# Seven products instead of eight in seven down-projection chunks of a decoder layer

## The chip, the cores and the metric

The kernel runs on one core of a Trainium2 chip. The metric is device time in microseconds (us) of one execution, the median of several; lower is better. Beside the timed runs there is one profiled execution, in which every instruction's start and duration is recorded. PE is TensorE (the matrix engine), PEld its weight loads, DVE is VectorE, ACT is ScalarE, POOL is GpSimd, SP is SyncE, which here issues the weight loads from memory.

## The reference

One decoder layer over 256 tokens of width 2048 in 32-bit floats: two groups of attention heads, an output projection, and an MLP with squared ReLU. Cut to what matters:

```python
h = rms_norm(x, norm1_g)
proj = h @ w_in                      # 2048 -> 6152: q, k, v of both groups, 8 forget logits
...                                  # forgetting attention, dilated attention
mixed = concatenate([rms_norm(y_a, outnorm_a_g), rms_norm(y_b, outnorm_b_g)])
x = x + mixed @ w_out                # 2048 -> 2048
h = rms_norm(x, norm2_g)
x = x + square(relu(h @ w_mlp_in)) @ w_mlp_out     # 2048 -> 8192 -> 2048
return rms_norm(x, final_norm_g)
```

The MLP holds the largest share of the arithmetic: 2 x 2048 x 8192 weights against 256 tokens.

## The kernel before

**Arithmetic.** Every large product is done in three terms. A 32-bit operand is split into a high part (a copy in the type float32r) and a low part, the rest. A product is then high x high + low x high + high x low, three TensorE instructions that add up in PSUM. For each step of weights ScalarE copies the raw weights into the high tile `whi` (line 178), and VectorE subtracts to get the low tile `wlo` (line 179).

**Chunks and steps.** The work on TensorE is a list of chunks (lines 111 to 128). A chunk is 512 output columns over up to 16 feature tiles of 128. First come 12 chunks of q, v and k, then 8 of the output projection, then the MLP in four rounds (r = 0 to 3). Each round has four up chunks `u` that make 2048 hidden features, then four down chunks `d` that multiply these by 2048 rows of the down weights and add the result to the residual `xs`. A step is two feature tiles of one chunk. A raw load brings four feature tiles (1 MB) into one of four `wraw` buffers.

**Two forms of product.** In q, k and u chunks (`turned_product`, line 327) the weights are loaded into the array as 128x128 blocks and 256 tokens of activations are streamed: 12 products of 256 columns per feature tile. In v, o and d chunks (`product`, line 319, lines 323 to 325) the activations of one 128-token tile are loaded and 512 weight columns are streamed: 2 token tiles x 3 terms = 6 products of 512 columns per feature tile. In the last chunk the second token tile is done in two halves of 256 columns.

**Order.** The loop at the end (lines 780 to 793) writes out the order by hand. Before the products of step i it issues the split of step i + 3 (`LEAD`), so the four buffers of `wsplit` hold the current step and the three next; then the products of step i, and after each of the two feature tiles the side work that was filed for that place (`at`, `run_side`). Side work includes the drains: `drain_u` (line 620) takes relu on ScalarE, the square on VectorE and splits the hidden activations into `hT_hi`, `hT_lo` (the memory of `big_hi`, `big_lo` in the profile). `drain_d` adds a finished down chunk to `xs` with one VectorE instruction per token tile (`add_down`, line 648); in the last round it also sums squares on ScalarE and multiplies by the final gain. The gain row `gf` uses the memory of `relT` and is loaded by `load_gf` in the last round's first down chunk. The last chunk (`last_chunk`) and `finish` end the kernel.

**PSUM.** There are eight banks of 512 columns: four named `acc` for chunks (two per chunk), two `sc` and two `tr` that attention uses and that stand empty in the MLP.

Of the kernel before, what the change touches and what calls it, by code (L numbers as in the profile page):

```python
# [19 lines left out]
P = 128  # L20
# [22 lines left out]
LINE, NEAR, HIGH, LOW, GATED = 64, 8, 24, 56, 48  # L43
TURNED = "qku"
# [29 lines left out]
def kernel(  # L74
# [32 lines left out]
    dram = ctx.enter_context(tc.tile_pool(name="dram", bufs=1, space=DRAM))  # L107
    ctx.enter_context(tc.manual_schedule())
# [14 lines left out]
    ROUNDS = D_FF // D_MODEL  # L123
    for r in range(ROUNDS):
# [6 lines left out]
    steps, last_slot = [], {}  # L131
    for ci, (what, key, w, r0, c0, cols, kts) in enumerate(chunks):
        for s in range(kts // 2):
            steps.append((ci, s))
        last_slot[what, key] = 2 * len(steps) - 1

    raws, splits = {}, {}

    def load(i):
        if i >= len(steps) or steps[i][1] % 2 or (steps[i][0], steps[i][1] // 2) in raws:  # L140
            return
        ci, s = steps[i]
        _, _, w, r0, c0, cols, _ = chunks[ci]
        t = wraw.tile([P, 4, CW + NH], F32, name="raw")
        src = w[r0 + s * 256:r0 + s * 256 + 512, c0:c0 + cols].rearrange("(k p) c -> p k c", p=P)
        raws[ci, s // 2] = t
        if i == 0:
            return t, src
        n = 2 if i == 2 else 4
        for k in range(0, 4, n):  # L150
            nc.sync.dma_start(t[:, k:k + n, :cols], src[:, k:k + n])

    def split(i, j0=0, n=2):
        if i >= len(steps):
            return
        if j0:
            return split_rows(i, j0, n)
        ci, s = steps[i]
        if ci == len(chunks) - 1 and s < 4:
            hi, lo = (a[:, 4 * s:4 * s + 4, :].rearrange("p (k j) s -> p k (j s)", k=2) for a in (aT_hi, aT_lo))  # L160
        else:
            what, cols = chunks[ci][0], chunks[ci][5]
            high, low = (HIGH, LOW) if what in TURNED else (NEAR, NEAR) if cols == CW else (GATED, HIGH - NEAR)
            hi, lo = (
                wsplit.tile([P, 2 * CW + LINE], F32R, name=n)[:, b:b + 2 * cols].rearrange("p (j c) -> p j c", j=2)
                for n, b in (("whi", high), ("wlo", low))
            )
        splits[i] = (hi, lo)
        split_rows(i, j0, n)

    def split_rows(i, j, n):
        ci, s = steps[i]
        hi, lo = (a[:, j:j + n, :] for a in splits[i])
        t = raws[ci, s // 2][:, 2 * (s % 2) + j:2 * (s % 2) + j + n, :chunks[ci][5]]
        cols = t.shape[2]
        step = cols // 2 if i == j == 0 else cols
        for c in range(0, cols, step):
            nc.scalar.activation(hi[:, :, c:c + step], t[:, :, c:c + step], AF.Copy)  # L178
        nc.vector.tensor_tensor(lo, t, hi.bitcast(F32), op=ALU.subtract)  # L179
# [42 lines left out]
    pick_sb = two.tile([P, RW], F32, name="pr")[:N_BUCKETS + 1]  # L222
# [12 lines left out]
    gcat = one.tile([P, TB, P], F32R, name="gcat")  # L235
# [108 lines left out]
    def products(i, j):  # L344
        ci, s = steps[i]
        what, key, _, _, _, cols, kts = chunks[ci]
        kt = 2 * s + j
        if what in TURNED:
            return turned_product(ci, i, j, kt, kts)
        a = operands(what, key)  # L350
        if cols > CW:
            return gated_products(ci, i, j, kt, kts, a)
        if kt == 0:
            accs[ci] = [psum.tile([P, CW], F32, name="acc", bufs=4) for _ in range(TB)]
        go, end = kt == 0, kt == kts - 1
        for t in range(TB):
            product(accs[ci][t], a, kt, t, splits[i], j, slice(0, CW), go, end)

# [18 lines left out]
    lf = two.tile([P, 2, 3 * P], F32R, name="p")  # L377
# [30 lines left out]
    gate_s = one.tile([P, SEQ], F32R, name="gate_s")  # L408
    gate_t = one.tile([P, SEQ], F32R, name="gate_t")
# [19 lines left out]
    relT = one.tile([P, NH, SEQ], F32, name="relT")  # L429
    rel_d = dram.tile([NH, RW], F32, name="rel_d")  # L430

    def rel_row():
        p = psum.tile([P, 512], F32, name="sc")
        nc.tensor.matmul(p[:NH, :RW], relx, pick_sb, start=True, stop=True)
        row = two.tile([P, RW], F32, name="neg")[:NH]
        nc.vector.tensor_copy(row, p[:NH, :RW])
        nc.gpsimd.dma_start(rel_d, row)
# [16 lines left out]
    def drain_v(g, ci):  # L454
        acc = accs.pop(ci)
        vh = one.tile([P, TB, CW], F32R, name="v_hi")
        vl = one.tile([P, TB, CW], F32R, name="v_lo")
# [12 lines left out]
    rows1 = one.tile([P, SEQ], F32, name="rows1")  # L470
# [11 lines left out]
    def drain_qk(g, what, ci, half):  # L482
        if half == 0:
            qkv[g, what] = one.tile([P, 2, 4, SEQ], F32R, name=what)
# [15 lines left out]
    def decay_of(hd):  # L500
        decay[hd] = two.tile([P, SEQ], F32R, name="gate_h")
# [6 lines left out]
    def scores(g, h):  # L508
# [25 lines left out]
        neg = two.tile([P, 3 * P], F32, name="neg")  # L534
        pr = two.tile([P, 3 * P], F32, name="pr")
# [19 lines left out]
    def turn_probs(g, h):  # L555
# [4 lines left out]
        parts = two.tile([P, 2, 3 * P], F32R, name="p")  # L560
# [3 lines left out]
    sq = [one.tile([P, SEQ], F32, name=f"sq{k}") for k in range(2)]  # L564
    seen = [0, 0]

    def values(g, h):
# [13 lines left out]
        s = sq[kind] if first else two.tile([P, SEQ], F32, name="sqt", bufs=1)  # L581
# [38 lines left out]
    def drain_u(c, ci):  # L620


        acc = accs.pop(ci)
        for half in range(2):
            h = two.tile([P, CW], F32, name="nat")
            nc.scalar.activation(h, acc[half], AF.Relu)
            nc.vector.tensor_tensor(h, h, h, op=ALU.mult)
# [4 lines left out]
            )  # L632

    gf = relT.rearrange("p h s -> p (h s)")
# [4 lines left out]
    def load_gf():  # L639
        nc.sync.dma_start(  # L640
            gf, bass.AP(tensor=final_norm_g.tensor, offset=final_norm_g.offset, ap=[[0, P], [1, D_MODEL]])
        )
# [4 lines left out]

    def add_down(acc, t, cs, n):
# [4 lines left out]
        if n is not None:  # L653
            unused = two.tile([P, CW], F32, name="nat")
            unused, xc, total = unused[:, :cs.stop - cs.start], xs[:, t, cs], ssq3[:, t, n:n + 1]
            if cs.stop < D_MODEL:
                nc.scalar.activation(unused, xc, AF.Square, accum_out=total)
                put_gain(t, cs)
            else:
                nc.vector.tensor_tensor_reduce(unused, xc, xc, 1.0, 0.0, ALU.mult, ALU.add, total)  # L660

    def put_gain(t, cs):
        nc.vector.tensor_tensor(xs[:, t, cs], xs[:, t, cs], gf[:, cs], op=ALU.mult)
# [51 lines left out]
    for ci, (what, key, *_rest) in enumerate(chunks[:-1]):  # L715
# [33 lines left out]
        elif what == "u":  # L749
            at(e, drain_u, key[1], ci)  # L750
        else:
            at(e, drain_d, *key, ci)
            if key == (ROUNDS - 1, 0):
                at(e - 8, load_gf)
# [27 lines left out]
    done = 10  # L782
    for i in range(final):
        if i:
# [39 lines left out]
```

## Time and profile before

| what | value |
|---|---|
| timed runs, median of 3 (range) | 1104.29 us (1103.9 to 1106.22) |
| profiled execution, first to last instruction | 1214.1 us |
| granted TensorE clock in the profile, mean | 0.850 of full speed |
| PE busy | 1201.8 us (99%) |
| VectorE busy | 655.5 us (54%) |
| ScalarE busy | 521.1 us (43%) |
| moved from and to memory | 209.17 MB, mean 172 GB/s |

The profiled execution's own time is its span; no other time is given for it. It is longer than the timed runs. In the rows of the profile `out<-in` names the tiles that an instruction writes and reads, `L340` is line 340 of the kernel before, and `x768` counts instructions. A matmul's duration (some 290 ns for 256 columns) is longer than its share of the array, since matmuls overlap; the pace is read from the starts of successive ones.

### The profile page before, as it was taken

The numbers are of one execution on the slowest core, as the hardware profiler recorded it, in microseconds if no ns is written. First come the engines' busy times: TensorE is split into PE (matmuls) and PEld (weight loads), VectorE is DVE, ScalarE is ACT, GpSimd is POOL, SyncE is SP. The second block draws the span as 40 slices with busy tenths as digits, with TensorE's granted clock in tenths as the row PEclk, the third lists the DMA queues.
The fourth block names the chain that finished last, engine by engine and source line by source line (L and its number), as shares of the span: only waits on it lengthen the run. The fifth ranks groups of instructions, "written<-read, shape, count | busy, mean of one in ns | idle before, by whom it ended". The sixth has DMA issues, their size and how long they took to land.

```text
span 1214.1 us, 17573 instructions
## 1 busy us (share of the span) xinstructions
PE 1201.8 (99%) x7373; PEld 1070.3 (88%) x7373; DVE 655.5 (54%) x837; ACT 521.1 (43%) x687; POOL 27.3 (2%) x42
## 2 busy tenths in 40 slices
PE   9999999999999999999999999999999999999997
PEld 8999898998987799987789997779998779998776
DVE  5666656556566655544544455445545444555563
ACT  5454535445444544443334443334444333444341
POOL 0010200000000000000000000000000000000000
PEclk8888888888888888888888888888888888888887
DMA  8664553544544455555555545555655555545541
GB/s 300 200 209 139 169 178 112 190 160 139 184 153 165 148 174 173 161 187 175 176 175 175 173 170 187 179 170 158 194 183 178 174 173 173 174 147 222 187 139 70
DMA packets 105387, 209.17 MB, mean 172 GB/s; under 512 B 3971, under 2 KB 5084, under 8 KB 105180
## 3 DMA queue, kind: packets, MB, share of 16 engines
q1 hardware_dynamic: 104412, 206.59, 51.6%
q8 instruction: 57, 0.93, 0.3%
q0 software_dynamic: 304, 1.06, 0.2%
q10 hardware_dynamic: 592, 0.40, 0.1%
q14 instruction: 22, 0.18, 0.0%
HBM read 205.93 MB, written 2.11 MB: 171 GB/s over the span
## 4 chain that ended last, share of the span: by engine, by line
PE 99%; DMA 0%; DVE 0%; issue 0%; ACT 0%; POOL 0%; ACTq 0%; DVEq 0%
PE acc L340 48%; PE acc L324 16%; PE acc L323 16%; PE acc L325 16%; PE tr L275 1%; PE sc L575 1%; PE sc L531 0%; PE tr L559 0%; DMA xs<-in_x_dram 0%; PE sc L527 0%; PE sc L577 0%; PE sc L323 0%; PE sc L324 0%; PE sc L325 0%; PE sc L521 0%
## 5 line engine op out<-in xcount | busy, mean ns | idle before, releaser
L179 DVE TENSOR_TENSOR wlo<-raw,whi 128x1024 fp32r<-128x1024 f32 (+2 forms) x382 | 464.0, 1223 | 416.9 <-ACT whi L178 414.8
L178 ACT ACTIVATE whi<-raw 128x1024 fp32r<-128x1024 f32 (+2 forms) x383 | 398.7, 1051 | 475.0 <-PE acc L340 230.1
L340 PE MATMUL acc<-aT_hi,whi 128*128 128x256 f32 x1536 | 450.5, 294 | 0.0
L340 PE MATMUL acc<-aT_hi,wlo 128*128 128x256 f32 x1536 | 446.3, 291 | 0.0
L340 PE MATMUL acc<-aT_lo,whi 128*128 128x256 f32 x1536 | 445.7, 291 | 0.0
L340 PEld LDWEIGHTS acc<-aT_hi,whi 128*128 128x128 f32 x1536 | 306.0, 199 | 1.5 <-ACT p L261 0.7
L340 PEld LDWEIGHTS acc<-aT_lo,whi 128*128 128x128 f32 x1536 | 304.8, 199 | 0.4
L340 PEld LDWEIGHTS acc<-aT_hi,wlo 128*128 128x128 f32 x1536 | 304.9, 199 | 0.0
L324 PE MATMUL acc<-whi,big_lo 128*128 128x512 f32 (+1 forms) x632 | 262.4, 415 | 0.0
L323 PE MATMUL acc<-whi,big_hi 128*128 128x512 f32 (+1 forms) x632 | 262.2, 415 | 0.0
L325 PE MATMUL acc<-wlo,big_hi 128*128 128x512 f32 (+1 forms) x632 | 260.6, 412 | 0.0
L323 PEld LDWEIGHTS acc<-whi,big_hi 128*128 128x128 f32 x632 | 121.6, 192 | 36.1
L325 PEld LDWEIGHTS acc<-wlo,big_hi 128*128 128x128 f32 x632 | 121.6, 192 | 35.9
L324 PEld LDWEIGHTS acc<-whi,big_lo 128*128 128x128 f32 x632 | 121.7, 193 | 34.6
L323 PE MATMUL acc<-whi,aT_hi 128*128 128x512 f32 (+1 forms) x144 | 54.7, 380 | 0.0
L324 PE MATMUL acc<-whi,aT_lo 128*128 128x512 f32 (+1 forms) x144 | 54.1, 376 | 0.0
L325 PE MATMUL acc<-wlo,aT_hi 128*128 128x512 f32 (+1 forms) x144 | 54.1, 376 | 0.0
L262 DVE TENSOR_TENSOR big_lo<-nat,big_hi 128x512 fp32r<-128x512 f32 x32 | 22.2, 692 | 22.4 <-ACT big_hi L261 22.4
L650 DVE SCALAR_TENSOR_TENSOR xs<-acc,rstd2sq,xs 128x512 f32<-128x512 f32 (+1 forms) x33 | 24.2, 734 | 16.2 <-PE acc L325 16.2
L325 PEld LDWEIGHTS acc<-wlo,aT_hi 128*128 128x128 f32 x144 | 27.7, 192 | 5.5
L323 PEld LDWEIGHTS acc<-whi,aT_hi 128*128 128x128 f32 x144 | 27.9, 194 | 5.2
L324 PEld LDWEIGHTS acc<-whi,aT_lo 128*128 128x128 f32 x144 | 27.9, 194 | 5.1
(167 smaller groups left out, 508.4 us busy)
## 6 DMA issues: line engine op xcount, KB each, us to landing
raw<-in_w_mlp_in_dram SPq DMA_DIRECT2D x64, 1024.0 KB, 5.3
raw<-in_w_mlp_out_dram SPq DMA_DIRECT2D x64, 1024.0 KB, 5.1
raw<-in_w_in_dram SPq DMA_DIRECT2D x42, 1024.0 KB, 5.0
raw<-in_w_out_dram SPq DMA_DIRECT2D x16, 1024.0 KB, 5.1
raw<-in_w_in_dram SPq DMA_DIRECT2D x4, 1040.0 KB, 8.1
xs<-in_x_dram SPq DMA_DIRECT2D x3, 512.0 KB, 9.8
raw<-in_w_in_dram SPq DMA_DIRECT2D x2, 512.0 KB, 5.7
big_lo<-rel_d POOLq DMA_DIRECT2D x1, 1024.0 KB, 7.0
```

Source lines behind the costliest of these rows:

```text
L178: nc.scalar.activation(hi[:, :, c:c + step], t[:, :, c:c + step], AF.Copy)
L179: nc.vector.tensor_tensor(lo, t, hi.bitcast(F32), op=ALU.subtract)
L262: nc.vector.tensor_tensor(lo, src, hi.bitcast(F32), op=ALU.subtract)
L275: nc.tensor.transpose(p[:, j * SEQ + t * P:j * SEQ + (t + 1) * P], xs[:, t, c:c + P], ident)
L323: nc.tensor.matmul(acc, xh, hi[:, j, cols], start=go, stop=False, skip_group_check=True)
L324: nc.tensor.matmul(acc, xl, hi[:, j, cols], start=False, stop=False, skip_group_check=True)
L325: nc.tensor.matmul(acc, xh, lo[:, j, cols], start=False, stop=end, skip_group_check=True)
L340: nc.tensor.matmul(acc, w[:, j, b * P:(b + 1) * P], a[:, kt, :], start=kt == 0 and b % 2 == 0 and n == 0, stop=kt == kts - 1 and n == 2, s ...
L575: nc.tensor.matmul(y[:, :SEQ], v[:, 0, dims], p[:, m, :SEQ], start=n == 0, stop=False, skip_group_check=True)
L650: nc.vector.scalar_tensor_tensor(xs[:, t, cs], acc[:, :cs.stop - cs.start], rstd2sq[:, t:t + 1], xs[:, t, cs], op0=ALU.mult, op1=ALU.add)
```

## The change

Seven of the 16 down chunks are computed by Strassen's scheme in its variant with 15 additions: d(0,0), d(1,0), d(2,0) and d(0,1), d(1,1), d(2,1), d(3,1). In these chunks four feature tiles, 256 tokens and 512 columns make a unit. It is cut into halves: two feature tiles (k1, k2), two token tiles (lower, upper), two column halves of 256. Where the plain form makes eight products of halves, the new form makes seven, with sums and differences of weight halves and of activation halves as operands. Each of these is again done in three terms.

A unit has four steps. **near** takes the k2 weights as they are (two products), **first** the left half of the k1 weights (one), **odd** two differences of weight halves (two), **even** two more (two). The differences are made by VectorE in a tile `both`: one instruction of 1024 elements at near, and two of 512 in place after odd has been split. The sums of activations are made once per up chunk by VectorE in place (`mix_activations`, four instructions of 256) and are split into `mix_hi`, `mix_lo` (`split_mixed`). The square in `drain_u` moves from VectorE to ScalarE.

The seven products add up in four banks, the two `sc` and the two `tr`, and `drain_seven` adds them to `xs` in four parts.

The order of steps changes. The units of d(r-1,0) are interleaved with the second halves of the up chunks of round r, one unit for each. Within a round d(r,3) comes first, then the units of d(r,1), each with two plain steps of d(r,2) between its steps; in the last round d(3,0) and d(3,3) follow as plain chunks.

Buffers: the attention tiles move into a pool of their own, which is closed where the MLP begins. Its memory then holds a fifth pair of split buffers, `mix_hi`, `mix_lo`, `both`, one small pair for first, and later the gain row. Splits are issued as far ahead as five large buffers (and one small) allow, and raw loads as soon as one of the four raw buffers is spent. `load_gf` moves to after the drain of d(3,1). In the last chunk three steps instead of four use the memory of `aT_hi`, `aT_lo`. The diff, cut to its core:

```diff
+    def mixed(ci, unit, behind):
+        b, a, t13, t24 = ((ci, 2 * unit, sub) for sub in ("near", "first", "odd", "even"))
+        return [b, a, t13, behind[0], t24] + behind[1:]
+
+    for r in range(ROUNDS):
+        for c in range(4):
+            mine = plain(index["u", (r, c)])
+            steps += mine[:4] + (mixed(index["d", (r - 1, 0)], c, mine[4:]) if r else mine[4:])
+        late = [index["d", (r, c)] for c in range(4)]
+        if r < ROUNDS - 1:
+            steps += plain(late[3])
+        for unit in range(4):
+            steps += mixed(late[1], unit, plain(late[2])[2 * unit:2 * unit + 2])
+        if r == ROUNDS - 1:
+            steps += plain(late[0]) + plain(late[3])
...
+    def split_seven(i):
+        ci, s, sub = steps[i]
+        t = raws[ci, s // 2][:, :, :CW]
+        half = CW // 2
+        if sub == "near":
+            both = sums_of[ci, s] = late_tiles["pool"].tile([P, 2, CW], F32, name="both")
+            nc.vector.tensor_tensor(halves(both), t[:, :, half:].rearrange("p (f k) c -> p f k c", f=2),
+                                    halves(t[:, :2]), op=ALU.subtract)
+        if sub == "first":
+            hi, lo = (late_tiles["pool"].tile([P, CW + LINE], F32R, name=n)[:, b:b + CW]
+                      for n, b in (("fhi", NEAR), ("flo", NEAR)))
+            src = t[:, :2, :half]
+        else:
+            hi, lo = part_tiles(i, 2 * CW, NEAR, NEAR)
+            src = t[:, 2:] if sub == "near" else sums_of[ci, s]
+        hi, lo = (a.rearrange("p (k c) -> p k c", k=2) for a in (hi, lo))
+        splits[i] = (hi, lo)
+        nc.scalar.activation(hi, src, AF.Copy)
+        nc.vector.tensor_tensor(lo, src, hi.bitcast(F32), op=ALU.subtract)
+        if sub == "odd":
+            a, b = src[:, :, :half], src[:, :, half:]
+            nc.vector.tensor_tensor(a, t[:, 2:, half:], a, op=ALU.subtract)
+            nc.vector.tensor_tensor(b, t[:, 2:, :half], a, op=ALU.subtract)
+            spent.add((ci, s // 2))
...
+    def seven_products(i, j):
...
+        todo = {
+            "near": ((one_, 0, h, k2, lower), (one_, half, m, k2, lower)),
+            "first": ((three, 0, h, k1, lower),),
+            "odd": ((two_, half, m, k2, upper), (four, 0, m, k1, upper)),
+            "even": ((three, half, m, k1, lower), (two_, 0, h, k2, upper)),
+        }[sub]
...
+            for x, (a, w) in enumerate(((ah, hi), (al, hi), (ah, lo))):
+                nc.tensor.matmul(acc, a[:, k, tokens], w[:, j, n * half:(n + 1) * half], start=fresh and x == 0,
+                                 stop=s == KT // 2 - 2 and j == 1 and x == 2, skip_group_check=True)
...
-            nc.vector.tensor_tensor(h, h, h, op=ALU.mult)
+            nc.scalar.activation(h, h, AF.Square)
...
+    def mix_activations(c):
+
+        a, b = kept[c]
+        (a11, a21), (a12, a22) = ((x[:, :, :P], x[:, :, P:]) for x in (a, b))
+        nc.vector.tensor_tensor(a22, a21, a22, op=ALU.add)
+        nc.vector.tensor_tensor(a21, a11, a21, op=ALU.subtract)
+        nc.vector.tensor_tensor(a11, a22, a11, op=ALU.subtract)
+        nc.vector.tensor_tensor(a12, a12, a11, op=ALU.subtract)
...
+        if part == 0:
+            s = late_tiles["pool"].tile([P, 2, half], F32, name="copies")
+            late_tiles["copies"] = s
+            nc.scalar.activation(s[:, 0], three[:, left], AF.Copy)
+            nc.scalar.activation(s[:, 1], four[:, left], AF.Copy)
+            nc.vector.tensor_tensor(rest, rest, s[:, 0], op=ALU.add)
+            add(0, cs, one_)
+        elif part == 1:
+            add(0, cs, three)
+            add(0, slice(cs.start + half, cs.stop), two_[:, right])
+        elif part == 2:
+            nc.vector.tensor_tensor(rest, rest, late_tiles["copies"][:, 1], op=ALU.add)
+            add(1, cs, two_)
+        else:
+            add(1, cs, rest[:, None, :].to_broadcast([P, 2, half]))
...
+            at(e + 2, mix_activations, key[1])
+            at(e + 4, split_mixed, key[1])
+        elif ci in seven:
+            for part in range(4):
+                at(e + 1 + 2 * part, drain_seven, *key, ci, part)
+            if key[0] == ROUNDS - 1:
+                at(e + 7, load_gf)
+                for c in (1, 2):
+                    for t in range(TB):
+                        at(e + 11 + 2 * c + t, put_gain, t, slice(c * CW, (c + 1) * CW))
...
+    def free_tiles(i):
+        live = [steps[n][2] for n in range(i, done + 2) if not (steps[n][0] == len(chunks) - 1 and steps[n][1] < 3)]
+        return len([n for n in live if n != "first"]) <= 5 and live.count("first") <= 1
...
+        if i >= mlp_start:
+            load_more()
+            while free_tiles(i) if i + LEAD < final else done < upto.get(i, i + LEAD):
+                done += 1
+                split(done)
+                load_more()
+            for j in range(2):
+                products(i, j)
+                run_side(2 * i + j)
+            continue
```

More of the change, by code (lines that the diff above doesn't have):

```diff
@@ L163, in split @@
             high, low = (HIGH, LOW) if what in TURNED else (NEAR, NEAR) if cols == CW else (GATED, HIGH - NEAR)
[L164 to L167, printed above, removed]
+            hi, lo = (a.rearrange("p (j c) -> p j c", j=2) for a in part_tiles(i, 2 * cols, high, low))
         splits[i] = (hi, lo)
@@ L559, in turn_probs @@
             nc.tensor.transpose(p[:, j * P:(j + 1) * P], pr[:, j * P:(j + 1) * P], ident)
-        parts = two.tile([P, 2, 3 * P], F32R, name="p")
+        parts = mix.tile([P, 2, 3 * P], F32R, name="p", bufs=2)
         split_psum(parts[:, 0], parts[:, 1], p[:, :3 * P])
         turned[g, h] = parts
-    sq = [one.tile([P, SEQ], F32, name=f"sq{k}") for k in range(2)]
+    sq = [mix.tile([P, SEQ], F32, name=f"sq{k}") for k in range(2)]
     seen = [0, 0]
```

149 lines of the change are left out of this document (115 added, 34 removed).

## The prediction

> **What bounds the kernel now.** I read the page first (busy times, granted clock, chain), then the waits, then two stretches of the MLP side by side, then the groups of instructions by shape, then the timeline at single places. The page:
>
> ```profile
> span 1214.1 us, 17573 instructions
> PE 1201.8 (99%) x7373; PEld 1070.3 (88%) x7373; DVE 655.5 (54%) x837; ACT 521.1 (43%) x687; POOL 27.3 (2%) x42
> PE 99%; DMA 0%; DVE 0%; issue 0%; ACT 0%; POOL 0%; ACTq 0%; DVEq 0%
> ```
>
> TensorE is busy 1201.8 of 1214.1 us and carries 99% of the chain that ended last. A busy PE need not be at its peak, so I look at pace. In the chain of waits, and in windows over the third round (its four up chunks, then its four down chunks) and over three other stretches (columns: us, then busy us and instructions of PE, PEld, DVE, ACT, POOL, then granted clock, DMA share, GB/s):
>
> ```profile
> 627.47 96.33 PE acc L340 x768
> ...
> 100.00:200.00 100.00, 100.00 (x692) 93.75 (x692) 61.98 (x116) 47.90 (x86) 8.19 (x9) 0.85 0.47 156
> 600.00:700.00 100.00, 100.00 (x690) 93.61 (x689) 48.98 (x46) 39.85 (x42) 0.00 (x0) 0.85 0.57 177
> 627.47:723.80 96.33, 96.33 (x769) 96.33 (x769) 47.85 (x47) 40.72 (x45) 0.00 (x0) 0.85 0.55 176
> 723.80:820.13 96.33, 96.33 (x386) 73.82 (x386) 46.93 (x43) 35.67 (x36) 0.00 (x0) 0.85 0.53 173
> ```
>
> Four up chunks are 768 products of 256 columns in 96.33 us: 0.12543 us each. Four down chunks are, by the code, 4 x 96 = 384 products of 512 columns, also in 96.33 us: 0.25086 us each, exactly twice. Time goes by columns streamed, at one clock (0.85), with no visible charge per instruction or per weight load. The timeline of the last chunk, second token tile, shows the form that the change uses (activations loaded, 256 weight columns streamed); first and last of its 96 products:
>
> ```profile
> 1193.24 0.30 PE L323 MATMUL acc<-aT_hi,big_hi 128*128 128x256 f32 x1
> ...
> 1205.17 0.28 PE L325 MATMUL acc<-wlo,big_hi 128*128 128x256 f32 x1
> ```
>
> (1205.17 - 1193.24)/95 = 0.1256 us: the same pace. So fewer streamed columns mean less time, as long as split weights are ready. That they are now, the waits show (us in total, times, longest; the first three are all that PE has, none in the MLP):
>
> ```profile
> PE tr L479 <- DVE nat L478: 1.3, 1, 1.3
> PE tr L275 <- DMA xs<-in_x_dram: 1.2, 1, 1.2
> PE sc L242 <- DVE relx L219: 1.2, 1, 1.2
> ...
> DVE wlo L179 <- ACT whi L178: 414.8, 312, 2.1
> ACT whi L178 <- PE acc L340: 230.1, 129, 2.1
> ACT whi L178 <- PE acc L324: 222.3, 124, 2.4
> SPq L151 <- DVE wlo L179: 1032.4, 180, 9.7
> ```
>
> Everything behind PE waits for PE: ScalarE for a free split buffer, VectorE for ScalarE, the load queue for VectorE.
>
> **The removal.** A unit is four feature tiles of one chunk. Plain: 4 x 2 token tiles x 3 terms = 24 products of 512 columns, 24 x 0.25086 = 6.02 us. As seven products: near 12, first 6, odd 12, even 12 = 42 of 256 columns, 42 x 0.12543 = 5.27 us. Saved 0.7526 us; 7 chunks x 4 units = 28 units: **21.07 us** of profile time. PE gets 28 x 18 = 504 instructions more, each with a weight load; by the two paces above these are free.
>
> **The added work on VectorE and ScalarE.** Prices, from groups by shape, and from the timeline:
>
> ```profile
> L179 DVE TENSOR_TENSOR wlo<-raw,whi 128x1024 fp32r<-128x1024 f32 x370 | 451.5, 1229 | 412.5 <-ACT whi L178 410.8 <-DMA pk<-in_pack_dram 0.5
> L650 DVE SCALAR_TENSOR_TENSOR xs<-acc,rstd2sq,xs 128x512 f32<-128x512 f32 x31 | 23.2, 750 | 10.7 <-PE acc L325 10.6
> L262 DVE TENSOR_TENSOR big_lo<-nat,big_hi 128x512 fp32r<-128x512 f32 x32 | 22.2, 692 | 22.4 <-ACT big_hi L261 22.4
> L627 DVE TENSOR_TENSOR nat<-nat 128x512 f32<-128x512 f32 x32 | 22.0, 688 | 11.1 <-ACT nat L626 11.1
> ...
> L178 ACT ACTIVATE whi<-raw 128x1024 fp32r<-128x1024 f32 x370 | 387.6, 1057 | 466.7 <-PE acc L340 229.7 <-PE acc L324 222.3 <-issue 7.7
> L261 ACT ACTIVATE big_hi<-nat 128x512 fp32r<-128x512 f32 x32 | 20.3, 633 | 26.1 <-DVE nat L627 26.1
> L626 ACT ACTIVATE nat<-acc 128x512 f32<-128x512 f32 x32 | 18.9, 590 | 21.1 <-PE acc L340 21.1
> ...
> 1205.49 0.48 DVE L650 SCALAR_TENSOR_TENSOR xs<-acc,rstd2sq,xs 128x256 f32<-128x256 f32 x1 [4.21 <-PE acc L325]
> 1206.61 0.41 DVE L663 TENSOR_TENSOR xs<-xs,relT 128x256 f32<-128x256 f32 x1
> ```
>
> VectorE per mixed unit: both 1.229, four low parts of near, odd, even (3 x 1.229) and first (0.692), two in-place differences (2 x 0.688) = 6.98 us, against 2.46 for a plain unit. ScalarE: 3 x 1.057 + 0.633 = 3.80, against 2.11. The strided differences are not in the trace; they lie between the plain 128x1024 row (1.229) and twice the row that reads PSUM (2 x 0.750 = 1.50 for 1024). I take 1.229, since both are SBUF to SBUF in runs of 256.
>
> The tightest place is the second chunk of a round interleaved with two plain steps of the third. PE per unit: 5.27 + 2 x 3.01 = 11.29 us. VectorE: 6.98 + 2.46 = **9.44**; ScalarE 5.92. Among up chunks: PE 24.08 + 5.27 = 29.35; VectorE 8 x 1.229 + 6.98 + the drain (low parts 2 x 0.692, mixing 4 x 0.41, mixed low parts 2 x 0.692; the squares go to ScalarE) = 21.2; ScalarE 8 x 1.057 + 3.80 + 2 x 0.590 + 6 x 0.633 = 17.2. A seven-product drain costs VectorE 4 x 0.75 + 3 x 0.48 = 4.4 us, not 1.5. Over the MLP VectorE gains 28 x 4.52 + 16 x 1.65 + 7 x 2.9 = 173 us, to about three quarters of the stretch. All of it lies beside PE as long as the lead over PE holds. That lead, in a down chunk (ScalarE, then VectorE):
>
> ```profile
> 738.64 1.06 ACT L178 ACTIVATE whi<-raw 128x1024 fp32r<-128x1024 f32 x1 [1.95 <-PE acc L324]
> ...
> 739.73 1.22 DVE L179 TENSOR_TENSOR wlo<-raw,whi 128x1024 fp32r<-128x1024 f32 x1 [1.78 <-ACT whi L178]
> ```
>
> PE frees a buffer at 738.6; it is refilled at 740.95 and used three steps later, at 738.6 + 3 x 3.01 = 747.6: 6.7 us to spare. Afterwards five buffers cover the five large operands of a unit. Near, freed 1.5 us into a unit, has its high part at 2.6 and its low part (both ran earlier) at about 3.8, and is used at 11.29: 7.5 us to spare. The plain steps are tightest, 6 us. A drain waits for a step whose buffer the next split needs as well, so it holds nobody back for longer than its own 4.4 us. Cost: nothing; if the lead were gone, see the rivals.
>
> **Moves and waits.** Loads: two megabyte loads per 11.29 us where it was one per 6.02; both chunks share four raw buffers. The final gain is now loaded after the second chunk's drain, behind the raw loads on SP's queue, and its first reader on VectorE comes three plain steps (9 us) later:
>
> ```profile
> raw<-in_w_mlp_out_dram SPq DMA_DIRECT2D x64, 1024.0 KB, 5.1
> relT<-in_final_norm_g_dram SPq DMA_DIRECT2D x1, 1024.0 KB, 8.4
> ```
>
> 8.4 against 9 us: at worst a wait of a few us on VectorE with low parts queued behind it, inside the 6 us of lead. The sc and tr banks that hold the seven products are drained during the five plain steps (15 us) before the next unit needs them. Attention's tiles move to a pool whose memory the MLP takes over; they were last read eight output chunks earlier. The tail (1205.3 to 1214.1) and the head keep their instructions. I take 0 for all of these, with 0 to 2 us for the range.
>
> **Sum.** 1214.1 - 21.07 = 1193.0 us of profiled span. No longer time is given for the profiled execution. The timed runs (1103.9 to 1106.22) are shorter than its span: median/span = 0.9096. PE is 99% of the span, so this can only be a faster PE; read as clock, 0.85/0.9096 = 0.93. The saving scales to 19.2 us, **1085.1 us**. Bounds: unscaled 21.1 (1083.2); at full clock 21.07 x 0.85 = 17.9 (1086.4). Other engines do not speed up with PE: the tight unit becomes 11.29 x 0.9096 = 10.27 us against VectorE's 9.44, still 8% free.
>
> The Trainium skill ("TensorE: Matmul & The Clock Gate", section "Wait — 56ns, not 53.3ns?") gives each warm matmul a fixed cost of about 2.5 ns beside its columns, which speaks against replacing long products by more short ones. By it 504 more products would cost 1.3 us, an estimate, and the time would be about 1086.3. The trace disagrees, at 0.85 clock: 0.25086 is exactly twice 0.12543.
>
> **Rivals.**
>
> *VectorE falls behind in the tight stretches.* For: only 8% is free there, and the strided forms and nine handovers per unit have no row. Against: 6 to 7 us of lead at each entry. If its work there costs 15% more, 10.86 against 10.27, the 16 units lose 0.59 each, 9.4 us, the lead hiding none: 1094.5. Chance 0.14.
>
> *The lead is lost, and ScalarE and VectorE work in turn.* Place: the same 16 units; if the order of buffers makes each split wait for the product just before its use, a unit takes 5.92 + 9.44 = 15.36 instead of 10.27 us, 81 more in all: 1166. It turns the gain into a loss from 10.27 + 19.2/16 = 11.5 us per unit. Against: by the order above each buffer comes free five large steps before its use. Chance 0.05.
>
> *Weight loads come into view.* PEld is busy for all of an up stretch (96.33 of 96.33). If the mixed units went by the loads' mean instead of by columns, 42 x 28 x 0.192 = 226 us would replace 168.6; 52 more at timed pace: 1156. The gain is gone at 48/42 x 0.12543 = 0.143 us a product.
>
> ```profile
> L323 PEld LDWEIGHTS acc<-whi,big_hi 128*128 128x128 f32 x632 | 121.6, 192 | 36.1
> ```
>
> Against: loads overlap in the up chunks and in the last chunk, at 0.125. The same page says (section "Measured speedup vs the span model") that a load overlaps a running product only if the row groups differ. By that rule the loads would show here; the trace disagrees, 0.12543 us for a product and its load. Chance 0.03.
>
> *The clock pays.* More work on two engines lowers PE's granted clock by 1.8%: 1104.3. Against: VectorE at 62% and at 49% of a window stood beside the same 0.85. Chance 0.04.
>
> That fewer columns are not streamed at all I can exclude by the count: 168.6 us of products go, 147.5 come.
>
> **How the numbers follow.** Forecast 0.74; VectorE late 0.14; clock 0.04; lead lost 0.05; loads 0.03. Faster by over 0.2% (2.2 us, about what these runs can tell apart): 0.88; within: 0.04; slower: 0.08. The range goes from just under the unscaled saving, 1082, to the late VectorE, 1095; what lies beyond is the last three cases, 0.12, and little more.
>
> **What would show it.** Right: PE instructions 7373 + 504 = 7877; span near 1193; mixed products 0.125 us apart; no PE wait in the MLP; VectorE around 830 us busy (655.5 + 173); clock 0.85. A repeated PE wait on a low part at near or odd would show the lead too short; starts over 0.14 us apart, the loads; a clock under 0.84, the fourth rival. Any of these above 2 us in sum proves the zero costs wrong.

## The result and the profile after

The changed kernel takes 1099.22 us (median of 4 runs, 1097.77 to 1099.82), the kernel before 1104.53 (4 runs). The ratio is 0.9947, 95% interval 0.9933 to 0.9961: faster, by about 5 us and not by 19. It lies outside the range of 1082 to 1095. The head of the profile page and PE's list of waits, after (the waits: us in total, times, longest):

```profile
span 1096.0 us, 19064 instructions
PE 1080.1 (99%) x7877; PEld 1014.8 (93%) x7877; DVE 800.7 (73%) x1076; ACT 604.1 (55%) x821; POOL 27.9 (3%) x42
PEclk9999999999999999999999999999999999999999
```

```profile
PE tr L457 <- DVE xs L777: 3.3, 1, 3.3
PE tr L580 <- DVE nat L579: 1.4, 1, 1.4
PE sc L316 <- DVE relx L293: 1.2, 1, 1.2
PE tr L349 <- DMA xs<-in_x_dram: 1.1, 1, 1.1
```

The reader should see three things. PE has 7877 products, as counted. VectorE has grown to 800.7 us, less than the forecast 830. And the granted clock is at full speed (0.996 on average), where the trace of before stood at 0.85 throughout; that one profiled execution was slower than the timed runs. To compare like with like, the kernel before was profiled once more.

### The profile page after: what moved, and what is told of

It reads as the page before. It is cut to its first block, busy times and chain, and to the rows that moved or that the text cites. A ratio compares the mean times of both kernels' runs of the same rounds, so it can differ in the third digit from the quotient of the medians.

```text
span 1096.0 us, 19064 instructions
## 1 busy us (share of the span) xinstructions
PE 1080.1 (99%) x7877; PEld 1014.8 (93%) x7877; DVE 800.7 (73%) x1076; ACT 604.1 (55%) x821; POOL 27.9 (3%) x42
## 4 chain that ended last, share of the span: by engine, by line
PE 98%; ACT 0%; DVE 0%; DMA 0%; issue 0%; POOL 0%; ACTq 0%; DVEq 0%
PE acc L414 48%; PE acc L397 11%; PE acc L398 11%; PE acc L399 11%; PE sc L457 7%; PE tr L457 5%; PE tr L349 1%; PE sc L676 1%; PE sc L632 1%; PE tr L660 0%; DMA xs<-in_x_dram 0%; PE sc L628 0%; ACT whi L252 0%; PE sc L678 0%; PE sc L398 0%
## 5 line engine op out<-in xcount | busy, mean ns | idle before, releaser
L253 DVE TENSOR_TENSOR wlo<-raw,whi 128x1024 fp32r<-128x1024 f32 (+2 forms) x327 | 394.5, 1221 | 162.0 <-ACT whi L252 161.1
L252 ACT ACTIVATE whi<-raw 128x1024 fp32r<-128x1024 f32 (+2 forms) x328 | 339.2, 1050 | 228.3 <-PE acc L414 129.9
L397 PE MATMUL acc<-whi,big_hi 128*128 128x512 f32 (+1 forms) x414 | 160.2, 387 | 0.0
L398 PE MATMUL acc<-whi,big_lo 128*128 128x512 f32 (+1 forms) x414 | 159.9, 386 | 0.0
L399 PE MATMUL acc<-wlo,big_hi 128*128 128x512 f32 (+1 forms) x414 | 159.8, 386 | 0.0
L399 PEld LDWEIGHTS acc<-wlo,big_hi 128*128 128x128 f32 x414 | 78.1, 189 | 15.8
L398 PEld LDWEIGHTS acc<-whi,big_lo 128*128 128x128 f32 x414 | 78.1, 189 | 14.4
L397 PEld LDWEIGHTS acc<-whi,big_hi 128*128 128x128 f32 x414 | 78.1, 189 | 14.2
L218 ACT ACTIVATE whi<-both 128x1024 fp32r<-128x1024 f32 x56 | 59.7, 1066 | 49.0 <-DVE both L223 17.1
L219 DVE TENSOR_TENSOR wlo<-both,whi 128x1024 fp32r<-128x1024 f32 x56 | 68.3, 1220 | 4.7 <-ACT whi L218 3.8
L335 ACT ACTIVATE mix_hi<-nat 128x512 fp32r<-128x512 f32 x32 | 18.5, 625 | 29.9 <-DVE nat L745 29.9
```

Source lines behind the costliest of these rows:

```text
L218: nc.scalar.activation(hi, src, AF.Copy)
L219: nc.vector.tensor_tensor(lo, src, hi.bitcast(F32), op=ALU.subtract)
L335: nc.scalar.activation(hi, src, AF.Copy)
L397: nc.tensor.matmul(acc, xh, hi[:, j, cols], start=go, stop=False, skip_group_check=True)
L398: nc.tensor.matmul(acc, xl, hi[:, j, cols], start=False, stop=False, skip_group_check=True)
L399: nc.tensor.matmul(acc, xh, lo[:, j, cols], start=False, stop=end, skip_group_check=True)
```

## The experiments

Times are medians of timed runs with the ratio to the kernel before on the same chip, or a single time. The labels in brackets (c1, e1 and so on) are the names by which the expectations refer to runs. Where a pace is given in tenths of ns, it is the mean distance between successive products' starts in the trace.

**The kernel before again** (c1). No edit.

> The kernel before, unchanged, for a trace at the clock of the timed runs (the trace of before stood at 0.85, that of the changed kernel at 1.00). If PE's time went by columns alone at every clock, 256-column products come every 106.7 us/1000 at full clock (0.12543 x 0.85) and the span would be near 1035 us. If something beside the clock limits them, as the changed kernel's rows say (113.3 ns for the up chunks' products, 226.7 for the 512-column ones), the span is 1100 to 1104 us and these two paces show here too, with 256-column products of the last chunk at 120 ns.

Measured: 1105.58 us, granted clock 0.998. Windows over the second round's up chunks, then its down chunks (the same stretches as 627.47 to 820.13 in the prediction, which are the second round and not the third; columns as there; the counts take in a few products at the edges), and the first and last product of the second token tile in the last chunk:

```profile
span 1103.8 us, 17573 instructions
571.83:658.89 87.06, 87.06 (x769) 87.06 (x769) 47.53 (x47) 40.82 (x45) 0.00 (x0) 1.00 0.62 195
658.89:745.95 87.06, 87.06 (x386) 72.09 (x386) 46.45 (x43) 35.69 (x36) 0.00 (x0) 1.00 0.59 193
...
1083.16 0.28 PE L323 MATMUL acc<-aT_hi,big_hi 128*128 128x256 f32 x1
...
1094.55 0.28 PE L325 MATMUL acc<-wlo,big_hi 128*128 128x256 f32 x1
```

At the clock of the timed runs an up product of 256 columns takes 87.06/768 = 113.4 ns, a down product of 512 columns 87.06/384 = 226.7. If time went by columns alone at every clock, the first would be 125.43 x 0.8504 = 106.7 (0.8504 is the unrounded clock of that trace). And the last chunk's products, the very form of the seven, take (1094.55 - 1083.16)/95 = 119.9 ns, not half of 226.7. At 0.85 the trace had shown 125.4 and 125.6 for the two: the slower clock covered a charge beside the columns that the faster one lays open, and the charge differs between the two.

**Halving the products, with nothing else added** (e3). In the kernel before, each plain down product becomes two.

```diff
+            if what == "d":
+                for c0 in (0, CW // 2):
+                    product(accs[ci][t][:, c0:c0 + CW // 2], a, kt, t, splits[i], j, slice(c0, c0 + CW // 2),
+                            go and c0 == 0, end)
+                continue
             product(accs[ci][t], a, kt, t, splits[i], j, slice(0, CW), go, end)
```

> The kernel before, but in 15 down chunks each 512-column product is issued as two of 256 columns with the same loaded activations (1440 more products, no other work more). By columns alone: no change. If each 256-column product costs 120 ns against half of 226.7: 2 x 1440 x 6.7 ns = 19 us slower than before, about 1123 us. No work on VectorE or ScalarE is added, so a slower pace here would not be contention with added work.

Measured: 1122.74 us, 17 to 18 more than before. 80 us of a pure down stretch:

```profile
490.00:570.00 80.00, 80.00 (x669) 80.00 (x668) 38.31 (x34) 29.43 (x28) 0.00 (x0) 1.00 0.59 195
```

80 us hold some 667 products: 120.0 ns each, with VectorE under half busy. So this form of product pays the charge here with no added work beside it: two halves cost 240.0 ns, the whole 226.7.

**The wait of the last round, taken away** (e1). The chain of waits of the changed kernel around 1000 us (start, us, what), and windows over the same place:

```profile
994.94 0.61 ACT nat L728
995.58 0.64 ACT nat L729
996.24 0.64 ACT big_hi L335
996.88 0.49 ACT nat L728
997.39 0.64 ACT nat L729
998.08 0.51 issue
998.59 1.05 ACT whi L252
999.66 1.23 DVE wlo L253
1000.89 0.67 DVE xs L777
1001.61 0.70 PE tr L457 x3
...
985.00:994.90 9.90, 9.90 (x89) 9.90 (x88) 9.83 (x12) 5.32 (x7) 0.00 (x0) 1.00 0.73 249
994.90:1001.60 6.70, 3.40 (x28) 3.03 (x26) 5.87 (x10) 5.51 (x8) 0.00 (x0) 1.00 0.27 104
1001.60:1005.00 3.40, 3.39 (x13) 3.10 (x14) 3.30 (x6) 2.16 (x4) 0.00 (x0) 0.56 0.79 267
1002.10:1005.30 3.20, 3.20 (x13) 2.81 (x12) 3.13 (x5) 2.46 (x4) 0.00 (x0) 0.50 0.84 308
```

The last up chunk's drain occupies ScalarE from 994.9 (relu L728, square L729, high part L335, twice). Behind it on ScalarE stands a split (`whi` L252), behind that on VectorE its low part (L253), and behind that the fourth part of the drain of d(2,0) (L777), which frees the bank that d(3,1) needs. In earlier rounds the plain chunk d(r,3), 22 us long, and three up steps lie between the last product of d(r-1,0) and the first of d(r,1); in the last round only the three up steps do. VectorE has no room left: 9.83 of 9.90 us just before. The wait costs twice, since after it PE runs at half clock for some 3.4 us (0.50 in the last window, 0.56 where the window begins a little earlier). The edit files the parts one feature tile apart for this one drain:

```diff
-                at(e + 1 + 2 * part, drain_seven, *key, ci, part)
+                at(e + 1 + (part if key == (ROUNDS - 2, 0) else 2 * part), drain_seven, *key, ci, part)
```

> The changed kernel, but the four parts of the drain of d(2,0) filed one after another (one feature tile apart instead of two), so that the last part stands ahead of the last up chunk's drain. Theory 'one stall': PE waits 3.3 us for that part and then runs a window of 3.4 us at half clock; without the wait both go, and the kernel is 4.5 to 5.5 us faster than the changed one, about 1094 us, ratio to before 0.990. Rival 'contention': PE is slowed everywhere by VectorE's and ScalarE's work, the wait only moves to the next product: at most 2 us faster, ratio 0.993 or more.

Measured: 1093.58 us, ratio 0.9899 (0.9886 to 0.9912), 5.6 us below the changed kernel. PE's waits:

```profile
PE tr L349 <- DMA xs<-in_x_dram: 1.4, 1, 1.4
PE tr L580 <- DVE nat L579: 1.4, 1, 1.4
PE sc L316 <- DVE relx L293: 1.2, 1, 1.2
PE acc L399 <- DVE wlo L253: 0.4, 1, 0.4
```

The 3.3 us are gone, 0.4 us is left behind a low part, and the rival, a stall that only moves on, is out.

**Is the pace of the seven contention with VectorE?** (e7) On top of the earlier drain all VectorE work of the mixed units is left out: raw halves stand for the differences, the high part for the low one.

```diff
-            both = sums_of[ci, s] = late_tiles["pool"].tile([P, 2, CW], F32, name="both")
-            nc.vector.tensor_tensor(halves(both), ...
+            sums_of[ci, s] = t[:, :2]
...
-        splits[i] = (hi, lo)
+        splits[i] = (hi, hi)
         nc.scalar.activation(hi, src, AF.Copy)
-        nc.vector.tensor_tensor(lo, src, hi.bitcast(F32), op=ALU.subtract)
-        if sub == "odd":
...
+        if sub == "even":
             spent.add((ci, s // 2))
```

> The changed kernel with the earlier drain, leaving out all of VectorE's work in the mixed units: no differences of weight halves (raw halves stand in their place) and no low parts (the high part stands in their place), 6.98 us less of VectorE for each of 28 units; same products, same loads, same ScalarE work. Theory 'contention': plain 512-column products between them go from 230 to 226.7 ns and the seven products from 118.4 to 113.3: 7 us faster than 1093.6, about 1086.5. Theory 'addresses' without contention: the seven products stay at 118 to 120 ns, 1093 to 1095 us, and the plain 512-column products at 230.

Measured: 1095.35 us, no gain. The four mixed units of d(0,1), first with the earlier drain alone, then without VectorE's work:

```profile
504.65:546.59 41.94, 41.94 (x265) 37.92 (x264) 34.37 (x36) 23.38 (x26) 0.00 (x0) 1.00 0.63 199
```

```profile
507.70:549.64 41.94, 41.94 (x265) 37.91 (x264) 14.60 (x14) 23.32 (x26) 0.00 (x0) 1.00 0.68 222
```

VectorE falls from 34.4 to 14.6 us, and PE needs the same 41.94 us for the same products. Contention with VectorE is out as the cause, for the pace of the seven (118.4 ns in both runs) and for that of the 512-column products between them (228.6 ns on average, up to 236). The same rows show that VectorE is no bound here.

**Where operands start** (e2, e4, e5). Three runs move operands within a 64-word line. In the changed kernel and in the plain down chunks weights start 8 words past a multiple of 64, and so do the plain activations; in up chunks the loaded weights start at 24 and 56 and the streamed activations at 8.

```diff
-            hi, lo = part_tiles(i, 2 * CW, NEAR, NEAR)
+            hi, lo = part_tiles(i, 2 * CW, HIGH, LOW)
...
-MIX_HI, MIX_LO = 24, 32
+MIX_HI, MIX_LO = 8, 0
```

> The changed kernel, but the split operands of the seven products start 24 (high) and 56 (low) words past a multiple of 64 instead of 8, and both mixed activation tiles start at 8 as the plain ones do. Theory 'addresses': a streamed and a loaded operand that start at the same place of a 64-word line cost 120 ns per 256-column product, and 16 or 48 words apart 113.3; then all seven products go to 113.3, 1176 x 5 = 6 us faster than the changed kernel, about 1093 us. Rival 'form': loaded activations cost 118 to 120 wherever they start: no change, 1099 us. Rival 'contention': no change in the mixed units either, since VectorE does the same work.

Measured: 1096.79 us, ratio 0.9928 (0.9915 to 0.9941). The seven go from 118.4 to 117.7 ns, near falls from 1.42 to 1.41 us per 12 products. That is under 1 us; the trace does not show the rest of the 2.4 us between the medians. The wait of 3.3 us is still in this kernel, and its runs spread from 1094.97 to 1098.6. The same offsets in the halved kernel before:

> The kernel before with halved down products (1440 more, 120.0 ns each in the run without offsets), and now the split down weights start 24 (high) and 56 (low) words past a multiple of 64 instead of 8; the loaded activations start at 8. No work on VectorE or ScalarE is added, so contention with added work plays no part. Theory 'addresses': what a product pays beside its columns depends on where the two operands start in a 64-word line; the pace falls as in the changed kernel with these offsets (117.7 ns on average) or to 113.3, and the time from 1122.7 to about 1116 or 1104 us. Rival 'form': 120.0 ns as without offsets, 1122.7 us. Rival 'contention' (that the 117.7 of the mixed units is 113.3 plus VectorE's traffic): 113.3 here, 1104 us.

Measured: 1117.81 us, 118.3, 118.3 and 116.7 ns for the three terms, close to those of the changed kernel with these offsets (118.3, 118.0 and 116.8). So places do act, alone and without contention, but by 2 ns of the expected 7. And both edits together:

> The changed kernel with both the earlier drain of d(2,0) (5.6 us by itself) and the offsets of the seven products' operands (2.4 us by itself). If they are independent, as two theories of different places would have it: 1099.2 - 8.0 = 1091.2 us, ratio to before 0.988. If the pace were limited by the same thing as the wait: no more than the larger, 1093.6 us, ratio 0.990.

Measured: 1093.77 us, ratio 0.9898 (0.9882 to 0.9915): no better than the earlier drain alone. The offsets' 2.4 us did not add up; by the traces they were never more than 0.8 us (139.2 us for all seven products, then 138.4).

**The order of the three terms** (e6, e6b, e8).

```diff
-            for x, (a, w) in enumerate(((ah, hi), (al, hi), (ah, lo))):
+            for x, (a, w) in enumerate(((ah, hi), (ah, lo), (al, hi))):
```

> The changed kernel with the earlier drain, and in the seven products the terms in the order high x high, high x low, low x high, so that the same loaded activations come twice in a row, as the same weights do in the up chunks (113.3 ns). Theory 'repeated load': what an up chunk's product saves comes from loading the same block twice: the triple falls from 355 to about 340 ns, 1176 x 5 = 6 us, 1088 us. Theory 'addresses': the order doesn't matter, 1093 to 1094 us.

Measured: 1091.22 us, and in timed rounds (below) 1090.86. Products with mixed activations, which start at 24 and 56, fall from 118.2 to 115.6 ns; those with plain ones, at the same place as the weights, stay at 118.5. Neither theory holds alone: order acts on the products whose activations start at 24 and 56, and not on the others.

> The run e6 again with timed rounds (earlier drain, new order in the seven products, all places as in the changed kernel). From its single time 1091.2 us; by its trace the seven products take 137.4 us instead of 139.2 with the old order, so 1.8 us less than the earlier drain alone: 1091 to 1092 us, ratio 0.988.

Measured: ratio 0.9878 (0.9864 to 0.9893), the fastest version here.

> The changed kernel with the earlier drain, the offsets of the run e2 (weights of the seven products at 24 and 56, all activations at 8) and the term order of e6. Theory 'where two operands start, in their order': the mean of the seven products changes again from the 117.7 of these offsets with the old order; if it follows the up chunks, whose two equal loads in a row go with 113.3, it falls to about 114.5, 1176 x 3.2 = 3.8 us, about 1090 us. Theory 'form': the mean stays between 116 and 118.5.

Measured: 1092.05 us, 117.4 ns, the "form" end. Weights and activations start at different places here too, and the order is worth 0.3 ns: that the places differ is not enough.

**Plain activations at 24 and 56 too** (e9, e10, e11). Two pads before `big_hi` and `big_lo`, with the earlier drain and the new order; a third keeps the tiles behind them in their places.

```diff
+    wide.tile([P, HIGH - NEAR], F32, name="pad_hi")
     yT_hi = wide.tile([P, 2 * NH, SEQ], F32R, name="big_hi")
+    wide.tile([P, LOW - HIGH], F32, name="pad_lo")
     yT_lo = wide.tile([P, 2 * NH, SEQ], F32R, name="big_lo")
```

> The changed kernel with the earlier drain and the term order of e6, and now the hidden activations of the plain form start 24 (high) and 56 (low) words past a multiple of 64, as the mixed ones do; all weights of down chunks stay at 8. In e6 the products with mixed activations run at 115.6 ns and those with plain ones, at the same place as the weights, at 118.5. Theory 'addresses': the 504 products with plain activations fall to 115 as well, 1.7 us, about 1089.5 us, and the 512-column products may change too. Rival 'PSUM banks or position in the unit make the difference': no change, 1091.2 us.

Measured: 1092.61 us, ratio 0.9886 (0.9873 to 0.99). Chain pieces of the third unit of d(0,1), near (12 products) and first (6), in the changed kernel and here:

```profile
525.73 1.42 PE sc L457 x12
527.15 0.71 PE tr L457 x6
```

```profile
527.72 1.38 PE sc L457 x12
529.10 0.68 PE tr L457 x6
```

The seven now run at 114.3 ns, nearly as the up chunks do: 134.4 us in all instead of 139.2 with the earlier drain alone. The last chunk shows the place alone: its second token tile has the form of the seven, and this run leaves its order of terms and its weights as they were. First and last of its 96 products:

```profile
1070.03 0.28 PE L397 MATMUL acc<-aT_hi,big_hi 128*128 128x256 f32 x1
...
1080.80 0.28 PE L399 MATMUL acc<-wlo,big_hi 128*128 128x256 f32 x1
```

(1080.80 - 1070.03)/95 = 113.4 ns, where it was 119.9 with the activations at 8. So in a long row of equal products the place of the loaded activations alone takes away what this form pays beyond an up product. In the mixed units it was not enough: the mixed activations start at 24 and 56 in the changed kernel too, and with the old order they took 118.2 ns. With the new order (e6) the twelve products of odd, all on mixed activations, take 118 to 122 ns for the first three and 113 to 114 for the rest, while in near and even, where mixed and plain activations take turns, most take 115 to 120. But the 512-column products rose from 228.7 to 231.7 ns and took back the same 4.8 us. The plain chunk d(1,3), with the earlier drain alone and here:

```profile
482.86:504.65 21.79, 21.79 (x99) 18.04 (x98) 17.15 (x21) 12.87 (x17) 0.00 (x0) 1.00 0.57 192
```

```profile
484.55:506.81 22.26, 22.26 (x99) 18.02 (x98) 17.21 (x21) 12.86 (x17) 0.00 (x0) 1.00 0.55 189
```

The new order for these too, and both moves in the kernel before:

> As e9, and the plain 512-column products too in the order high x high, high x low, low x high. They take 226.7 ns now, 13.3 more than twice the 106.7 that 256 columns take at the full clock. If their charge falls by as much as the 256-column products' does, some 6 ns for 1500 products: 9 us less than e9, about 1080 us. If a 512-column product hides what a load costs whatever its order: no change.

> The kernel before, without the seven products, with only these two moves: activations of the down and output chunks at 24 and 56, and the term order high x high, high x low, low x high. It tells what is left to the seven products once both kernels have them. If 512-column products don't respond: 1104 us, and e9 stands 14 us below it. If they respond as in the second case of e10, up to 14 us less than before, about 1090 us, and the seven products' own gain stays as in e10 against this.

Measured: 1092.59 us (0.9889, 0.9876 to 0.9903), no change, and 1113.59 us (1.0075, 1.0061 to 1.0089): the kernel before becomes slower, since its 1872 products of 512 columns in down and output chunks rise from 227.2 to 232.1 ns and it has few of the other form. A place that suits one form costs the other. With both moves in both kernels the seven products save 1113.59 - 1092.59 = 21.0 us. The paces there, 231.8 and 114.8 ns, give 28 x (24 x 231.8 - 42 x 114.8) = 20.8, so the two paces account for what the seven products save. Against the kernel before as it was, this version is no better than the earlier drain alone.

**Two maps** (m1, m2). The kernel before, each down chunk with its own start, both orders.

```diff
-            high, low = (HIGH, LOW) if what in TURNED else (NEAR, NEAR) ...
+            key = chunks[ci][1]
+            high, low = (8 * ((4 * key[0] + key[1]) % 8),) * 2 if what == "d" else (HIGH, LOW) ...
```

> The kernel before with halved down products (256 columns, activations at 8), each down chunk with its own start of both weight parts in a 64-word line: 0, 8, 16, ... 56 in rounds 0 and 1 with the old term order, the same again in rounds 2 and 3 with the order high x high, high x low, low x high. Nothing but places and order differs between chunks. Theory 'addresses': the pace differs from chunk to chunk between 113.3 and 120 ns, with 120 at 8 and less where the distance to the loaded block is 16 or 48; the start that gives 113.3, if there is one, would give the seven products their 6 us without moving the activations. Rival 'only a move of the activations helps': 117 to 120 ns in all chunks.

> The kernel before with the hidden activations at 24 (high) and 56 (low), as in the run where 512-column products rose from 226.7 to 231.7 ns and 256-column ones fell to 113.4, and each down chunk's 512-column weights at their own start 0 to 56, old order in rounds 0 and 1, new order in rounds 2 and 3. Theory 'addresses': some start brings 226.7 back (one as far from 24 and 56 as 8 is from 8 cannot serve both, so perhaps 228 to 230 only). Rival 'the activations' own place': 231 to 232 ns in all chunks, and the two forms can't both be fast.

Measured: 1120.33 us for the first map, 1116.13 for the second, one run each (mean ns of a product without a chunk's first 24; activations at 8 for the halves, at 24 and 56 for the 512 columns):

| start of the weights | 0 | 8 | 16 | 24 | 32 | 40 | 48 | 56 |
|---|---|---|---|---|---|---|---|---|
| 256 columns, old order | 118.3 | 120.0 | 117.8 | 117.8 | 120.0 | 118.6 | 117.4 | 117.8 |
| 256 columns, new order | 118.3 | 120.0 | 117.8 | 117.8 | 120.0 | 118.6 | 117.4 | |
| 512 columns, old order | 233.3 | 231.8 | 233.3 | 231.1 | 233.3 | 228.9 | 233.3 | 233.3 |
| 512 columns, new order | 233.3 | 231.9 | 233.3 | 231.1 | 233.3 | 233.3 | 233.3 | |

Places act chunk by chunk. For the halves, with activations at 8, the order changes nothing. No start of the weights gives 113.3 with activations at 8, and none gives 226.7 with activations at 24 and 56. One entry stands out, 228.9 at 40, and with the other order it isn't there. It was tried (f1):

> The run e9 (earlier drain, new order in the seven products, hidden activations at 24 and 56), and the plain weights of the down and output chunks start at 40 instead of 8, where the map gave 228.9 ns per 512-column product instead of 231.9. Theory 'addresses': 1499 products x 3 ns = 4.4 us less than e9 (1092.6), about 1088 us, ratio to before 0.985. Rival 'a chunk's pace in the map belongs to its place in the kernel': no change, 1092.6 us.

```diff
-            high, low = (HIGH, LOW) if what in TURNED else (NEAR, NEAR) ...
+            high, low = (HIGH, LOW) if what in TURNED else (40, 40) if what in "do" else (NEAR, NEAR) ...
```

Measured: 1093.29 us, 0.9898 (0.9882 to 0.9915), 512-column products at 232.4 ns. The entry did not carry over.

## Why the prediction was wrong

Direction and mechanism held: PE bounds the kernel, streams fewer columns, and the split operands arrive in time nearly everywhere. The size failed. At the paces of the timed clock the removal is 28 x (24 x 226.7 - 42 x 113.4) = 19.0 us, as much as the 19.2 forecast by scaling. 5.3 us were measured. Where the rest went:

| term | us | shown by |
|---|---|---|
| wait for a bank in the last round, and half clock after it | 5.6 | the earlier drain |
| the seven products at 118.4, not 113.4 ns (139.2 us for 133.3) | 5.9 | halving, places and order; not contention |
| 512-column products: 151.0 us less of them, not 152.4 (228.7 ns on average, 227.5 before) | 1.4 | the trace: the first nine after each mixed step; cause open |
| not placed | 0.8 | |

- **"By the two paces above these are free"**, of the 504 added products. This failed. The paces were read at a clock of 0.85. At the clock of the timed runs a product pays 6.7 to 13.3 ns beside 106.7 for 256 columns. I scaled the span, read the shorter time as a clock of 0.93 (the timed runs stood at 0.998), and so assumed that every form speeds up alike; the trace of before could not show otherwise, and its last chunk, my best row, was the form that speeds up least.
- **"Drained during the five plain steps (15 us) before the next unit needs them."** This failed. The five steps are those behind a second chunk d(r,1). Behind a first chunk there are three up steps and a plain chunk in rounds 1 and 2, and in the last round the three up steps alone, some 8 us, which the prediction did not look at. I costed the moves at 0, with 0 to 2 us for the range; this one was 5.6 us, because the drain stands on VectorE behind a low part, that behind ScalarE's split, and that behind the up chunk's drain, and because the wait halves the clock afterwards.
- **VectorE's price.** 800.7 us busy against 649.3 in the new trace of before: 151 us more, not 173. The price itself was right: the durations of its instructions add up to 846.1 us against 674.5, 172 more, but the records of successive ones overlap a little, and busy time counts an overlap once. That VectorE would be the bound of the tight units was a rival; its work taken away changed nothing there. But it was 9.83 of 9.90 us busy just before the wait.
- **The fixed cost per product** was weighed against a rule of the Trainium skill and set aside ("TensorE: Matmul & The Clock Gate", section "Wait — 56ns, not 53.3ns?"). The rule's direction was right: by this trace 5.9 us, where its 2.5 ns give 1.3. The row that seemed to refute it was one at a slower clock, and that section says of this cost that it shows only at the full clock of the array, which the prediction left out.
- **Weight loads in view, the clock, the lead lost**: the traces show full clock outside the wait's wake, products closer than the loads' mean duration of some 190 ns, and, once the drain is moved, no wait of PE over 0.4 us in the MLP. The rule on row groups that the prediction names stands on the same page under "The mechanism", not in the section given there. The exact rule behind the place of operands and the order of terms stays open. So does why 512-column products need up to 236 ns behind a mixed step. There the first nine take 226 to 236 ns and the rest 226 to 227, 1.2 us in all over 32 such places; the kernel before shows the like, up to 236 ns, where a down chunk follows an up chunk.

## What to carry to other kernels

Before trading few long products for more short ones, read the pace of both forms at the clock of the timed runs, in the very operand roles and places that the change will use; a trace at a lower clock can hide a charge per product. Follow each bank from its last product through every queue that its drain stands in, for the first and the last round as well, where the steps that cover it elsewhere may be missing.

## What the runs showed of the hardware

- At full granted clock a 256-column product with loaded activations took, in long rows of equal products, 113.4, 117.4 to 118.6, or 120.0 ns with nothing else changed than where the operands start in a 64-word line; a 512-column one 226.7 to 233.3. At 0.85 the forms did not differ: 125.4 and 125.6 ns for 256 columns, 250.9 for 512.
- One wait of 3.3 us was followed by some 3.4 us at half clock (0.50 from 1002.1 to 1005.3 us). The Trainium skill states this ("TensorE: Matmul & The Clock Gate", section "What's actually happening": half clock after an idle window of about 3.4 us), and the trace agrees, with a wait a little shorter than that.
- Products are slower for a while after the form changes: by position, the first nine 512-column products behind a mixed step took 226 to 236 ns on average over 32 places, from the tenth on 226 to 227. The first nine up products behind a mixed step took 114 to 119 ns, then 113 to 114.
